# A two-layer trunk on one core: every large tile moved to a 512-byte place in SBUF

## The chip, the core and the metric

The kernel runs on one core of a Trainium2 chip. The core has a matrix engine (TensorE; PE in the profile, PEld for its loads of weights), a vector engine (DVE), a scalar engine (ACT), GpSimd (POOL), the queue of SyncE (SP) that issues most transfers, and 16 DMA engines between DRAM and the on-chip memory SBUF. SBUF has 128 partitions; a tile has the same byte address in all of them. The metric is the device time of one execution in microseconds (us), the median of several.

## What is computed

A context of 256 tokens and 256 latent tokens, 1024 features each, pass two layers. Each layer is a half-step SwiGLU, a token mixer (layer 0: RG-LRU; layer 1: gated DeltaNet), and another half-step SwiGLU, each behind an RMSNorm with shift and scale:

```python
def swiglu(h, w_in, w_out):
    gu = h @ w_in
    return (jax.nn.silu(gu[..., :D_FF]) * gu[..., D_FF:]) @ w_out

for i in range(DEPTH):
    x = x + 0.5 * m[:, 0, 2] * swiglu(adaln(x, g_sub[i, 0], m[:, 0]), ffn_w_in[i, 0], ffn_w_out[i, 0])
    ...
    o = mixer(h, hc)                  # RG-LRU, or gated DeltaNet in column-major order
    x = x + m[:, 1, 2] * o
    x = x + 0.5 * m[:, 2, 2] * swiglu(adaln(x, g_sub[i, 2], m[:, 2]), ffn_w_in[i, 1], ffn_w_out[i, 1])
return rms_norm(x, g_final)
```

All is float32, D_FF is 2816, and the context takes the same steps except at the very end. Nearly all the arithmetic is products of a [128 features, tokens] tile with [128, 128] tiles of weights.

## The kernel before

**Products.** A float32 operand is kept as two float32r parts, high and low (class HL). A product of tiles is three matrix products in `mm3`, lines 293 to 295: high weights with high data, high weights with low data, low weights with high data. The weights are the stationary operand, 128 columns, loaded anew for each product (one PEld row for each PE row). The data is the moving operand: 512 columns (context and latents) in most of the kernel, 256 columns where only one of the two is worked on.

**Stages, in order of time.** The start (up to some 62 us) works out the first modulation vectors; then come the first SwiGLU (to some 400 us), the RG-LRU (to 620), two more SwiGLUs (to 1346), DeltaNet's projections, chunked recurrence and readout (to 1707), and the last SwiGLU over the latents alone (to 1906). In the profile's names the input products of a SwiGLU are `gu<-hh,wp` and `gu<-hl,wp`, its output products `fo` and `tl` (from `hidh`, `hidl`), DeltaNet's projections `f<-H,wp`, and the output projections of the mixers `op` and `tl` (from `grh`, `grl`, and from `y`).

**Weights.** A tile of weights is loaded by SP into a raw tile `wr` (line 218). ACT writes its high half-tile by a cast into `wp` (line 157, in `split`), and DVE writes the low one as the difference (line 158). Raw tiles and pairs come from two rings (class `Ring`): ring g lives for the whole kernel (3 raw tiles, 8 pairs), and ring l belongs to a stage (2 raw tiles, 6 pairs). There are two stages with a ring l: from the first SwiGLU to the one before DeltaNet, and the last SwiGLU. The strings given to `WS.cycle` say in which order the two rings are drawn from.

**Working tiles.** `slot` hands out [128, 512] tiles of a stage's pool (`hh`, `hl`, `hn`, `hidh`, `hidl`, `hf`, `sg`, `sq`, `uhh`, `grh` and so on). DeltaNet's normed stream `H` has a pool of its own; its readout keeps `S`, `y`, `kt`, and the small `so`, `ro`, `rq`, `jk`.

**Order.** The order on each engine is partly written out (`manual_schedule`) and partly the work of the layer that records the program; where that layer knows of fewer buffers it can choose another order. Where a tile lies in SBUF follows from the order in which the pools first hand out their tiles and from the tiles' sizes. No line of the kernel before asks for a particular place.

Of the kernel before, what the change touches and what calls it, by code (L numbers as in the profile page):

```python
# [25 lines left out]
# how far the parts of the work that share the engines run apart  # L26
PACE = {
    # RG-LRU: the order of the tiles, u and y of the input projection, g the gates
    "lru": "u0 u1 u2 u3 u4 u5 g0 u6 u7 g1 y0 y1 y2 g2 y3 y4 y5 g3 y6 y7",
    # DeltaNet: the order of the projections after the keys  # L30
    "seq": "qqqqqqqqvvvvzzvzzvvzzvzz",
    # the projections at which the decays begin and have to be done, and the keys' blocks begin
    "decay_from": 6, "decay_to": 8, "keys_from": 9,
    # steps per tick of the work behind the projections, and pauses in it
    "steps": 4, "decay_steps": 1, "key_every": 4, "key_steps": 3, "solve": 4, "q_lag": 2, "v_lag": 6, "k_lag": 4,
    # parts of the diagonal, and of the other blocks that the vector engine lays out; GpSimd has the rest
    "block_split": 1, "mo": 2,
    # the last heads of the groups that the readout's norms go in, and heads read out ahead of the projection
    "readout": "1 3 5 7", "heads": 4,
    # tiles of weights ready ahead of the projections  # L40
    "ahead": 1,
    # tiles of DeltaNet's weights that are kept in two parts: all projections from one on, so many of the output's;
    # and the places of FFNs (which, part, turns) in which that is done
# [3 lines left out]
# columns of the array of small constants  # L47
# [9 lines left out]
# columns of the array of masks (they depend on shapes alone)  # L57
# [12 lines left out]
class HL:  # L70
    """A float32 operand as two float32r parts whose sum is exact."""
# [11 lines left out]
class Parts:  # L83
    """two tiles [128, 256], indexed by the columns of either like one [128, 512]"""
# [10 lines left out]
def trunk(ctx, tc, io):  # L95
# [16 lines left out]
    @contextmanager  # L112
    def phase(ns, nraw=0, nw=0):
        """room for ns working tiles, and for more weights: nraw as loaded, nw halves of each part"""
        with tc.tile_pool(name=nm("ph"), bufs=1, reuse_waits="tile") as p:
            old = dict(scope)
            scope.update(s=p, ns=ns)
            if nw:
                ring_l = Ring(p, "l", nraw, nw)
                WS.cycle("glglglglglglgg", "gggl" if nraw == 1 else "gglgl", ring_l)  # L120
            else:
                WS.cycle("g", "g", None)
            yield
            scope.clear()
            scope.update(old)
# [20 lines left out]
    # ---------------------------------------------------------------- constants  # L146
# [8 lines left out]
    # ---------------------------------------------------------------- helpers  # L155
# [4 lines left out]
    class Ring:  # L160
        """room for weights: nraw as loaded, nw halves of each part"""
# [11 lines left out]
    class Weights:  # L173
        """the weights in the order of their use: first some tiles on their way, then in two parts"""

        def __init__(self):
            self.plan, self.raw, self.ready, self.todo = deque(), deque(), deque(), deque()
            self.rings = {"g": Ring(sb, "g", 3, 8)}
            # tiles that are brought into two parts where the engines have room for it, and kept in DRAM till their use
# [44 lines left out]
        def want(self, n, deep=True):  # L224
            """n tiles are to be ready; first halves first"""
# [20 lines left out]
        def step(self, n=1):  # L246
            """the next n halves"""
            self.put()
            while n and self.todo:
                raw, a, b, ring, r, parts = self.todo.popleft()  # L250
                w = self.rings[r[0] if r else next(self.next_pair)].pair()
                if b - a == 256:  # the decays' and betas' weights, 32 columns of both parts side by side
                    v = w.hi[:, :512].rearrange("p (k u x) -> p u k x", u=2, x=32)
                    split(HL(v[:, 0], v[:, 1]), raw[:, a:b].rearrange("p (k x) -> p k x", x=32))
                else:
                    split(w[:, :b - a], raw[:, a:b])
# [21 lines left out]
        def pop(self):  # L278
            """f(column) -> [128, 128] of the parts of the next tile"""
# [17 lines left out]
    def rsqrt_steps(y, v, n, short=False):  # L297
        """y = 1/sqrt(v) for small tiles [128, n]; short: fewer steps, with the scalar engine's help"""
# [20 lines left out]
    def run(it, n=None):  # L319
        """n steps of a generator, or all"""  # L320
# [9 lines left out]
    # ---------------------------------------------------------------- stream  # L330
    V2 = (0, 1)                       # 0: context, 1: latent
# [10 lines left out]
    # ---------------------------------------------------------------- adaLN vectors  # L342
    M = {}

    def finish_m(l, q, m, vs=V2, ts=slice(0, 8)):
        """m [128, 8, 2] holds silu(c) @ w of vector q; add the bias, and bring it to the form it is used in"""
# [17 lines left out]
    cs2 = cs.rearrange("p (k v) -> p k v", v=2)  # L364
    adap = tc.alloc_tile_pool(name="adap", bufs=1)
# [12 lines left out]
    def ada_tile(q, t, m, raw):  # L378
        """tile t of vector q of layer 0 on the tensor engine, from the rows of w; a generator of two steps"""
# [5 lines left out]
        x = small("adx", 128, 4)  # L385
# [7 lines left out]
    def ada_dot(t, m, raw, vs=V2):  # L393
        """tile t of a layer's vectors, from the columns of w"""
# [5 lines left out]
    class Ada:  # L400
        """the vectors that are not needed at the very start, tile by tile behind the SwiGLUs"""
# [11 lines left out]
        def step(self, n):  # L413
            """n more tiles; what is left of a fraction is kept"""
# [18 lines left out]
    # ---------------------------------------------------------------- norm + modulation  # L433
    class Norm:
        """RMSNorm of the stream with its modulation, piece by piece"""

        def __init__(self, l, s, perm=False, short=False):
            """short: nothing else to do while the norms are worked out"""
# [7 lines left out]
        def add(self, d, v):  # L446
            """d, v of the stream is final"""
# [11 lines left out]
        def ss(self, v):  # L459
            """1 / rms of each token; a generator of single steps"""  # L460
# [12 lines left out]
        def rr(self, v):  # L473
            """the same on all partitions"""
# [5 lines left out]
        def h(self, k, v):  # L480
            """tile k of the result; a generator of its two steps"""
# [16 lines left out]
    def first(norm, W, P, vs=V2):  # L498
        """the first matrix products of a phase, behind the norm: the context, then the latents"""
# [41 lines left out]
    def first_whole(norm, W, P, vs):  # L541
        """the same for context and latents together, with what the norm itself asks for"""
# [11 lines left out]
    def tail(ds, take, l, q, norm, vs, between=lambda more: None, split_=2, ahead=4, res=residual):  # L554
        """the last products of a phase, take() -> f(bank, columns, n of parts, part): the context is done first"""
# [60 lines left out]
    # ---------------------------------------------------------------- SwiGLU  # L616
# [85 lines left out]
    # ---------------------------------------------------------------- small helpers  # L702
    def log1p_steps(out, e, n):
        """log(1 + e) for 0 <= e <= 1, by 2 atanh(e / (2 + e))"""
# [28 lines left out]
    def out_proj(x, l, q, cols, norm, perm=False, ahead=4, before=lambda k: None):  # L733
        """stream += gate * (x @ w) over all output tiles"""
# [33 lines left out]
    def pause(n):  # L768
        """room for the engines' own queues between a result and what another engine does with it"""
# [3 lines left out]
    def conv(u, p, cw, vs=V2, bias=0.0):  # L773
        """u = 4-tap convolution over the tokens of each part; p: PSUM bank; a generator of two steps, and pauses"""
# [11 lines left out]
    # ---------------------------------------------------------------- RG-LRU  # L786
    class Pipe:
        """work on earlier tiles, in small steps behind the matrix products"""
# [17 lines left out]
    def project(w, x, dst, cols, tick=lambda: None, every=2):  # L806
        """dst[cols] of a bank = one tile of output features"""
# [5 lines left out]
    class Lru:  # L813
# [10 lines left out]
        def prepare(self):  # L824
# [4 lines left out]
            # log a = -4 sp (1 + th), th the tanh of half the gate's argument  # L829
# [106 lines left out]
    # ---------------------------------------------------------------- gated DeltaNet  # L936
    # Tokens are cut into chunks of 64; chunk i lies on the half i % 2 of the partitions, in slot
    # (i // 2) ^ (i % 2), so that step s of both directions works on the two halves of one slot.
# [809 lines left out]
```

## Time and profile before

| | |
|---|---|
| runs | 1915.66, 1916.98, 1919.57 us; median 1916.98 us |
| profiled execution | span 1917.1 us (no separate time is listed for it) |
| PE busy | 1855.7 us, 97% |
| PEld busy | 1583.3 us |
| DVE busy | 1319.2 us |
| ACT busy | 803.6 us |
| POOL busy | 89.3 us |
| HBM traffic over the span | 156 GB/s |

The span is the time from the first to the last instruction of one execution. Matrix products overlap: a product's own time in the profile (0.28 us for 256 columns at full clock, 0.39 us for 512) is longer than the step from its start to the next one's start, and the ends are modelled. The text therefore reads steps between starts: the time between two starts divided by the number of products that begin in between. One column in each cycle of the 2.4 GHz clock would be a step of 106.7 ns for 256 columns and of 213.3 ns for 512. The column PEclk is the granted clock, 1.00 for 2.4 GHz; during a stretch of half clock the products follow each other at 1.2 GHz.

### The profile page before, as it was taken

How to read it: one execution, taken by the hardware profiler on the slowest of the kernel's cores; microseconds unless marked ns; L12 is line 12 of the kernel's file. 1: busy time of each engine (PE TensorE's matmuls, PEld its weight loads, DVE VectorE, ACT ScalarE, POOL GpSimd, SP SyncE). 2: the span in 40 equal slices, each digit the busy share in tenths (PEclk: the TensorE clock that was granted, in tenths of full speed). 3: DMA queues.
4: the chain of work that ended last, by engine and by line, in shares of the span. 5: the costliest groups of instructions: out<-in, count | busy, mean ns of one | idle time of the engine just before them, and what ended most of it. 6: DMA issues, size and time to landing. Idle time of an engine off the chain costs nothing.

```text
span 1917.1 us, 29208 instructions
## 1 busy us (share of the span) xinstructions
PE 1855.7 (97%) x11078; PEld 1583.3 (83%) x11078; DVE 1319.2 (69%) x2772; ACT 803.6 (42%) x1651; POOL 89.3 (5%) x130
## 2 busy tenths in 40 slices
PE   5999999999999999999999999999999989989998
PEld 3788888898779888888898888888988987789997
DVE  7867766787888768766466555546765976975555
ACT  5522133257874432233333323323554332854444
POOL 3100000000000000000000000000012330100000
PEclk9999999999999999999999999999987979989999
DMA  9344644442323766566326665644223550035553
GB/s 334 132 159 158 214 169 161 156 170 78 99 76 134 233 230 218 187 217 220 126 86 214 225 207 210 208 144 139 83 78 101 169 173 1 1 101 184 189 179 108
DMA packets 98061, 300.54 MB, mean 157 GB/s; under 512 B 10880, under 2 KB 20352, under 8 KB 97792
## 3 DMA queue, kind: packets, MB, share of 16 engines
q1 hardware_dynamic: 92160, 277.69, 42.7%
q0 software_dynamic: 5760, 20.97, 3.5%
q8 instruction: 87, 1.43, 0.3%
q14 instruction: 54, 0.44, 0.1%
HBM read 276.61 MB, written 22.02 MB: 156 GB/s over the span
## 4 chain that ended last, share of the span: by engine, by line
PE 83%; DVE 9%; issue 3%; ACT 3%; DMA 1%; POOL 0%; SPq 0%; POOLq 0%; ACTq 0%; DVEq 0%
PE gu L294 14%; PE gu L293 14%; PE gu L295 14%; PE fo L294 4%; PE fo L293 4%; PE fo L295 4%; PE tl L294 4%; PE tl L293 4%; PE tl L295 3%; PE p L1408 1%; DVE u L781 1%; PE p L1397 1%; PE f L293 1%; PE gr L1069 1%; PE f L295 1%
## 5 line engine op out<-in xcount | busy, mean ns | idle before, releaser
L157 ACT CAST wp<-wr 128x512 fp32r<-128x512 f32 (+1 forms) x689 | 383.0, 607 | 308.8 <-DMA wr<-in_ffn_out_dram 59.8
L158 DVE TENSOR_TENSOR wp<-wr,wp 128x512 fp32r<-128x512 f32 (+1 forms) x689 | 433.3, 674 | 104.5 <-ACT wp L157 100.8
L294 PE MATMUL gu<-hl,wp 128*128 128x512 f32 (+1 forms) x1312 | 488.3, 372 | 7.2 <-DVE hl L495 7.2
L293 PE MATMUL gu<-hh,wp 128*128 128x512 f32 (+1 forms) x1312 | 485.5, 370 | 0.0
L295 PE MATMUL gu<-hh,wp 128*128 128x512 f32 (+1 forms) x1312 | 481.1, 367 | 0.0
L294 PEld LDWEIGHTS gu<-hl,wp 128*128 128x128 f32 x1312 | 248.7, 190 | 52.4 <-DVE hl L495 9.5
L293 PEld LDWEIGHTS gu<-hh,wp 128*128 128x128 f32 x1312 | 248.6, 189 | 49.1 <-ACT m L390 0.8
L397 DVE SCALAR_TENSOR_TENSOR junk<-ar,cb 128x1024 bf16<-128x1024 f32 x224 | 273.8, 1222 | 21.6 <-DMA ar<-in_w_adaT_dram 17.7
L295 PEld LDWEIGHTS gu<-hh,wp 128*128 128x128 f32 x1312 | 249.3, 190 | 45.2
L647 ACT ACTIVATE sg<-gu 128x512 f32<-128x512 f32 (+1 forms) x88 | 47.9, 545 | 385.9 <-PE gu L295 376.0
L649 DVE TENSOR_TENSOR hf<-sg,gu 128x512 f32<-128x512 f32 (+1 forms) x88 | 54.6, 620 | 198.7 <-PE gu L295 149.3
L293 PE MATMUL tl<-hidh,wp 128*128 128x256 f32 (+1 forms) x418 | 140.5, 336 | 0.0
L294 PE MATMUL tl<-hidl,wp 128*128 128x256 f32 (+1 forms) x418 | 140.5, 336 | 0.0
L295 PE MATMUL tl<-hidh,wp 128*128 128x256 f32 (+1 forms) x418 | 139.5, 334 | 0.0
L294 PE MATMUL fo<-hidl,wp 128*128 128x512 f32 (+1 forms) x352 | 129.4, 368 | 0.0
L293 PE MATMUL fo<-hidh,wp 128*128 128x512 f32 (+1 forms) x352 | 128.6, 365 | 0.0
L295 PE MATMUL fo<-hidh,wp 128*128 128x512 f32 (+1 forms) x352 | 128.1, 364 | 0.0
L293 PE MATMUL f<-H,wp 128*128 128x256 f32 x320 | 96.5, 301 | 1.4 <-ACT sq L1040 1.2
L295 PE MATMUL f<-H,wp 128*128 128x256 f32 x320 | 95.1, 297 | 0.0
L294 PE MATMUL f<-H,wp 128*128 128x256 f32 x320 | 94.9, 296 | 0.0
L293 PEld LDWEIGHTS tl<-hidh,wp 128*128 128x128 f32 x418 | 79.1, 189 | 9.3
L294 PEld LDWEIGHTS tl<-hidl,wp 128*128 128x128 f32 x418 | 79.2, 190 | 8.4
(327 smaller groups left out, 2904.9 us busy)
## 6 DMA issues: line engine op xcount, KB each, us to landing
wr<-in_ffn_in_dram SPq DMA_DIRECT2D x172, 512.0 KB, 4.6
ar<-in_w_adaT_dram SPq DMA_DIRECT2D x128, 512.0 KB, 3.7
wr<-in_ffn_out_dram SPq DMA_DIRECT2D x64, 512.0 KB, 4.9
kp<-wp SPq DMA_DIRECT2D x80, 256.0 KB, 7.2
wp<-kp POOLq DMA_DIRECT2D x40, 512.0 KB, 4.9
wr<-in_dn_in_dram SPq DMA_DIRECT2D x32, 512.0 KB, 3.9
wr<-in_ffn_out_dram SPq DMA_DIRECT2D x64, 192.0 KB, 3.5
wr<-in_lru_in_dram SPq DMA_DIRECT2D x16, 512.0 KB, 3.8
```

The costliest lines, as they stand in the source:

```text
L157: ACT.copy(dst.hi, src)
L158: DVE.tensor_tensor(dst.lo, src, dst.hi.bitcast(F32), OP.subtract)
L293: PE.matmul(out, w.hi, x.hi, start=start, stop=False)
L294: PE.matmul(out, w.hi, x.lo, start=False, stop=False)
L295: PE.matmul(out, w.lo, x.hi, start=False, stop=stop)
L397: DVE.scalar_tensor_tensor(junk, raw, 1.0, cb[:, v], OP.mult, OP.mult, accum_out=m[:, t % 8, v:v + 1])
L647: ACT.activation(sg[:, cols], P[0][:, cols], AF.Silu)
L649: DVE.tensor_tensor(hf[:, cols], sg[:, cols], P[1][:, cols], OP.mult)
L781: DVE.scalar_tensor_tensor(uv[:, :, a:b], pv[:, :, a + sh:b + sh], cw(j), uv[:, :, a:b], OP.mult, OP.add)
L1069: PE.matmul(gr[HI, o], gc[HI, c:c + 1].to_broadcast([64, 64]), ident[HI, HI], start=True, stop=True)
L1397: PE.matmul(p2[:, 0:128], Yp[a][:, j * 8 + hd, :], rr, start=True, stop=True)
L1408: PE.matmul(p3[dr][:, 0:128], KT[hd][r2[dr], j * 128:j * 128 + 128], vs[r2[dr]], start=True, stop=True)
```

## The change

Empty tiles (`pad`), a few changed sizes, and tiles handed out once and dropped (`slot("first")`, `ring_l.pair()`, `ring_l.raw()`) move the addresses at which the pools' tiles begin. The copies of ring l and the working tiles are now laid out in a fixed order at a stage's start: working tiles, pairs, raw tiles. Two sets of small buffers shrink: `adx` from 4 to 3, `jk` from 2 to 1. `ea` gets 16 columns instead of 64, of which it used 16. All comments are removed, which moves the line numbers (line 293 becomes 297). What is computed, and by which instructions, is the same.

```diff
     def phase(ns, nraw=0, nw=0):
...
             scope.update(s=p, ns=ns)
             if nw:
+                slot("first")
+            if nw:
                 ring_l = Ring(p, "l", nraw, nw)
+                ring_l.pair()
+                ring_l.raw()
                 WS.cycle("glglglglglglgg", "gggl" if nraw == 1 else "gglgl", ring_l)
...
     cs2 = cs.rearrange("p (k v) -> p k v", v=2)
+    new_m()
+    sb.tile([128, 112], F32, name="pad")
     adap = tc.alloc_tile_pool(name="adap", bufs=1)
...
-        x = small("adx", 128, 4)
+        x = small("adx", 128, 3)
...
-        y, sg, g, ea = (one(n, [128, 64], hp) for n in ("y", "sg", "g", "ea"))
+        y, sg, g = (one(n, [128, 64], hp) for n in ("y", "sg", "g"))
+        ea = one("ea", [128, 16], hp)
...
         KQ, QK, VN, Z, KT = ({} for _ in range(5))
+        one("pad", [128, 16])
...
         so, ro, rq = (rg.tile([128, 8, 2], F32, name=n) for n in ("so", "ro", "rq"))
+        rg.tile([128, 72], F32, name="pad")
...
-                jk = small("jk", 128)
+                jk = small("jk", 128, 1)
```

The places, as bytes past a multiple of 512, follow from the addresses in the two built programs:

| tile | before | after |
|---|---|---|
| pairs of weights, ring g (`wp`) | 64 | 0 |
| pairs of weights, ring l, first stage with one | 416 | 0 |
| pairs of weights, ring l, last SwiGLU | 64 | 0 |
| raw weights (`wr`), ring g and ring l of the last SwiGLU | 64 | 0 |
| raw weights, ring l of the first stage | 160 | 0 |
| working tiles (`hh`, `hl`, `hidh`, `hidl`, `grh` ...), first stage | 160 | 0 |
| working tiles, last SwiGLU | 64 | 0 |
| DeltaNet's normed stream (`H`) | 0 | 0 |
| readout's `y` and `kt`; `S` | 288 | 0 |
| DeltaNet's other large tiles (`kq`, `qk`, `u`, `vn`) | 384 | 384 |

The slices of weights that a product loads are 512 bytes wide and begin at multiples of 512 bytes within their tile, so a product's weights lie at the place of their ring.

On PE the order of the products is the same except in DeltaNet's readout, where the first output products (`op`) run between transposes of the last heads' results (`yt`). Before, transposes of two heads came after the first four products:

```order
L293 MATMUL op_15794<-y_15764,wp_13850 128x256
L293 MATMUL op_15795<-y_15764,wp_13925 128x256
L293 MATMUL op_15796<-y_15764,wp_13970 128x256
L293 MATMUL op_15797<-y_15764,wp_15115 128x256
L1456 MATMUL yt_15776<-ident,vn_13376 128x128 x2
L1456 MATMUL yt_15785<-ident,vn_13468 128x128 x2
L294 MATMUL op_15794<-y_15764,wp_13850 128x256
L295 MATMUL op_15794<-y_15764,wp_13850 128x256
```

Now they come twelve and thirteen products later:

```order
L298 MATMUL op_15804<-y_15771,wp_15122 128x256
L299 MATMUL op_15804<-y_15771,wp_15122 128x256
L297 MATMUL op_15801<-y_15780,wp_13856 128x256
L298 MATMUL op_15801<-y_15780,wp_13856 128x256
L299 MATMUL op_15801<-y_15780,wp_13856 128x256
L297 MATMUL op_15802<-y_15780,wp_13931 128x256
L1465 MATMUL yt_15783<-ident,vn_13382 128x128 x2
L298 MATMUL op_15802<-y_15780,wp_13931 128x256
L1465 MATMUL yt_15792<-ident,vn_13474 128x128 x2
```

The transposes moved; the number of products and transposes is the same.

On ACT, just ahead of that, the squares of the readout's norms (`jk`, two for each head) stood as pairs between the recurrence's own instructions (`vn`, `oq`):

```order
L1403 ACTIVATE vn_15546<-p_15544,btc 128x128
L1390 ACTIVATE oq_15540<-p_15534,egf 64x128 x2
L1437 ACTIVATE jk_15551,so<-vn_13266 128x128
L1437 ACTIVATE jk_15553,so<-vn_13266 128x128
L1390 ACTIVATE oq_15561<-p_15555,egf 64x128 x2
L1403 ACTIVATE vn_15567<-p_15565,btc 128x128
L1437 ACTIVATE jk_15572,so<-vn_13316 128x128
L1437 ACTIVATE jk_15574,so<-vn_13316 128x128
```

With one buffer for `jk` the second square of a head comes an instruction or more after the first:

```order
L1411 ACTIVATE vn_15553<-p_15551,btc 128x128
L1398 ACTIVATE oq_15547<-p_15541,egf 64x128 x2
L1446 ACTIVATE jk_15558,so<-vn_13272 128x128
L1411 ACTIVATE vn_15574<-p_15572,btc 128x128
L1446 ACTIVATE jk_15560,so<-vn_13272 128x128
L1398 ACTIVATE oq_15568<-p_15562,egf 64x128 x2
L1446 ACTIVATE jk_15579,so<-vn_13322 128x128
L1398 ACTIVATE oq_15609<-p_15603,egf 64x128
```

The recurrence's `vn` of a step moved ahead of the second square. DVE's small instructions of the same norms moved by a few places in the same way, and GpSimd and SP have the same order as before.

## Rows read from the trace of the kernel before

**Rows 1.** The page: span, busy time by engine, the chain by engine.
```profile
span 1917.1 us, 29208 instructions
PE 1855.7 (97%) x11078; PEld 1583.3 (83%) x11078; DVE 1319.2 (69%) x2772; ACT 803.6 (42%) x1651; POOL 89.3 (5%) x130
...
PE 83%; DVE 9%; issue 3%; ACT 3%; DMA 1%; POOL 0%; SPq 0%; POOLq 0%; ACTq 0%; DVEq 0%
```

**Rows 2.** Busy time by window: stretch, length, engines, PEclk, DMA share, GB/s.
```profile
62.00:240.00 178.00, 178.00 (x767) 143.51 (x766) 133.01 (x245) 53.10 (x97) 0.00 (x0) 1.00 0.52 176
...
400.00:620.00 220.00, 213.79 (x1203) 183.72 (x1203) 178.28 (x359) 149.34 (x255) 0.00 (x0) 1.00 0.32 106
620.00:970.00 350.00, 350.00 (x1586) 286.09 (x1585) 229.89 (x399) 117.91 (x212) 0.00 (x0) 1.00 0.60 205
...
1719.00:1906.00 187.00, 187.00 (x1560) 187.00 (x1560) 106.12 (x194) 87.77 (x180) 0.00 (x0) 1.00 0.49 164
```

**Rows 3.** PE's products by line and shape: count, busy us, mean ns.
```profile
L294 PE MATMUL gu<-hl,wp 128*128 128x512 f32 x992 | 397.7, 401 | 7.2 <-DVE hl L495 7.2
...
L294 PE MATMUL fo<-hidl,wp 128*128 128x512 f32 x264 | 104.5, 396 | 0.0
...
L294 PE MATMUL f<-H,wp 128*128 128x256 f32 x320 | 94.9, 296 | 0.0
...
L294 PE MATMUL gu<-hl,wp 128*128 128x256 f32 x320 | 90.6, 283 | 0.0
...
L294 PE MATMUL tl<-hidl,wp 128*128 128x512 f32 x198 | 78.4, 396 | 0.0
...
L294 PE MATMUL tl<-hidl,wp 128*128 128x256 f32 x220 | 62.1, 282 | 0.0
...
L536 PE MATMUL gu<-hl,wp 128*128 128x256 f32 x160 | 26.5, 289 | 0.4 <-DVE hl L495 0.4
...
L294 PE MATMUL fo<-hidl,wp 128*128 128x256 f32 x88 | 24.9, 283 | 0.0
```

**Rows 4.** PE's timeline, 512 columns, data at 160, weights at 416 (ring l).
```profile
175.56 0.39 PE L295 MATMUL fo<-hidh,wp 128*128 128x512 f32 x1
...
181.00 0.40 PE L295 MATMUL fo<-hidh,wp 128*128 128x512 f32 x1
```

**Rows 5.** PE's timeline, 512 columns, data at 160, weights at 64 (ring g).
```profile
193.74 0.39 PE L293 MATMUL fo<-hidh,wp 128*128 128x512 f32 x1
...
204.24 0.40 PE L293 MATMUL fo<-hidh,wp 128*128 128x512 f32 x1
```

**Rows 6.** PE's timeline, 512 columns, data at 160, both rings in turn.
```profile
250.09 0.39 PE L293 MATMUL gu<-hh,wp 128*128 128x512 f32 x1
...
268.30 0.39 PE L293 MATMUL gu<-hh,wp 128*128 128x512 f32 x1
```

**Rows 7.** PE's timeline, 256 columns, data at 0 (H), weights at 64.
```profile
1387.49 0.28 PE L295 MATMUL f<-H,wp 128*128 128x256 f32 x1
...
1403.59 0.28 PE L293 MATMUL f<-H,wp 128*128 128x256 f32 x1
```

**Rows 8.** The same shape and places, a little earlier.
```profile
1356.65 0.28 PE L533 MATMUL f<-H,wp 128*128 128x256 f32 x1
...
1370.66 0.28 PE L988 MATMUL ab<-H,wp 128*64 128x256 f32 x1
```

**Rows 9.** PE's timeline of the last SwiGLU, 256 columns, data and weights at 64.
```profile
1719.10 0.28 PE L532 MATMUL gu<-hh,wp 128*128 128x256 f32 x1
...
1906.04 0.28 PE L464 MATMUL ss<-ones,acc 128*128 128x1 f32 x2
```

**Rows 10.** PE's timeline, 256 columns, data at 160, weights at 416.
```profile
1330.11 0.28 PE L294 MATMUL tl<-hidl,wp 128*128 128x256 f32 x1
...
1341.74 0.28 PE L295 MATMUL tl<-hidh,wp 128*128 128x256 f32 x1
```

**Rows 11.** PE's timeline at half clock, 256 columns, data and weights at 64.
```profile
1716.19 0.41 PE L532 MATMUL gu<-hh,wp 128*128 128x256 f32 x1
...
1717.90 1.05 PE L536 MATMUL gu<-hl,wp 128*128 128x256 f32 x4
```

**Rows 12.** One tile's instructions (duration ns min/median/max): low weights, squares.
```profile
L158 DVE TENSOR_TENSOR wp<-wr,wp x689: 426/685/1643, 18.4 to 1900.9; 128x512 fp32r<-128x512 f32 x157, 128x384 fp32r<-128x384 f32 x15, 128x256 fp32r<-128x256 f32 x1
...
L1437 ACT ACTIVATION_READ_ACCUMULATOR jk<-vn x16: 186/190/193, 1668.5 to 1680.2; 128x1 f32 x16
```

## The prediction

> **What bounds the kernel now.** I read the page's busy times first: PE is busy for 1855.7 of 1917.1 us, and the chain that ends last runs 83% over PE [rows 1]. The windows then show where this is plain: in the first SwiGLU (62 to 240 us), in the second layer-0 SwiGLU and what follows (620 to 970 us) and in the last SwiGLU (1719 to 1906 us) PE is busy for the whole of the window, at full clock, while DVE is busy for 133 of 178, 230 of 350 and 106 of 187 us and the DMA engines for 0.49 to 0.60 of the time [rows 2]. In such a stretch a product that follows the one before it sooner shortens the end by as much, as long as the weights keep up. In the RG-LRU (400 to 620 us) PE has idle time and DVE is busy for 178 of 220 us; there I count no gain.
>
> So the question is the step from one product to the next. Four stretches without a pause, all at full clock, show that it isn't one number for one shape:
> - 512 columns, data at 160, weights at 416: 24 products from 175.56 to 181.00 us, a step of 226.7 ns [rows 4].
> - 512 columns, data at 160, weights at 64: 45 products from 193.74 to 204.24, 233.3 ns [rows 5]; with the rings in turn 78 from 250.09 to 268.30, 233.5 ns [rows 6].
> - 256 columns, data at 0, weights at 64: 142 products from 1387.49 to 1403.59, 113.4 ns [rows 7], but 119 from 1356.65 to 1370.66, 117.7 ns [rows 8].
> - 256 columns, data and weights both at 64: 1558 products from 1719.10 to 1906.04, 120.0 ns [rows 9]; data at 160 and weights at 416: 97 from 1330.11 to 1341.74, 119.9 ns [rows 10].
>
> One column a cycle would be 213.3 and 106.7 ns. The lowest steps of both shapes stand to these as 17 to 16 (226.7 and 113.3 ns), the others as 17.5 or 18 to 16. At half clock the excess is gone: 8 products from 1716.19 to 1717.90 take 213.8 ns each, where one column a cycle is 213.3 [rows 11]. So what costs is the supply of operands, not the array, and it depends on where data and weights lie to each other or to a boundary. This is what the change moves.
>
> **Beside a page.** The row says that the same shape at the same clock takes 113.4 or 120.0 ns by place. The Trainium skill (SBUF — State Buffer, Who interferes with whom) says that PE never waits on anyone and that its two read ports are independent; by it the places of data and weights would change nothing, and the sum below would be zero. The trace disagrees with it by those 6.6 ns, so the zero gets a small chance of its own.
>
> **The change part by part.** All products keep their number; only places, and a few instructions of the readout, move.
>
> 512 columns. The large groups are 992 x 3 input products and (264 + 198) x 3 output products, 2976 and 1386 [rows 3]. The input products draw on both rings in turn, at 233.5 ns; half of the output products are at 233.3, half at 226.7 after a few slower ones when the ring changes. No row has data and weights at 0. The nearest is rows 4: there data and weights are a multiple of 256 apart, as they are at 0 and 0, and the step is 226.7. With that: 2976 x 6.8 ns = 20.2 us, and 693 x 6.6 ns = 4.6 us, plus about 1 us for the slower ones at ring changes: 25.8 us less. From both sides: 240.0 ns would be 18 to 16, as the 256-column rows with equal places have it; 220.0 ns would be the least if the excess of rows 7 (6.7 ns) is one for each product and not for each column.
>
> 256 columns. The last SwiGLU has 1558 at 120.0 [rows 9]. The others of `gu`, `tl` and `fo` are (320 + 160) x 3 + 220 x 3 + 88 x 3 = 2364 in all, less these: 806, at about 118 to 120 [rows 3, 10]. If they come to 113.3: 1558 x 6.7 = 10.4 us, 806 x 5.5 = 4.4 us. DeltaNet's projections (320 x 3) keep data at 0; their mean own time of 296 ns against 283 for products at a step of 120 holds stalls and the half-clock stretches, so I read them by rows 7 and 8: a quarter at 117.7 that come to 113.3, 240 x 4.4 = 1.1 us. Together 15.9 us. Here the bounds are far apart: the two rows with equal places (9 and 10) both stand at 120, the one with data at 0 at 113.4. I take 113.3, because data at 0 is the only row in which the products reach it, and in rows 9 and 10 the data begins off a 512-byte boundary; the other reading is the first rival.
>
> Vector and scalar engines. The low halves of weights take 685 ns in the median whichever ring they are of [rows 12], so I put DVE and ACT at no change. They run beside PE: in the first SwiGLU DVE has 45 us in 178 to spare [rows 2], and a PE that is 3% faster uses 6 of them. If that cover were gone, the gain would stop at DVE's 133 us for this window, which is far off.
>
> Loads. The order on SP is as before, and with it what is queued behind each load. In the last SwiGLU ring l's raw tiles now lie where DeltaNet's Yp and the readout's first `y` were, so the second of them waits for the last product that reads that `y`, which is done before the last SwiGLU's first product. The order of DMAs behind it on SP waits too. I take 0.5 us, with 0 and 3 us as bounds.
>
> Readout. With one buffer for `jk`, ACT's second square of a head waits for the first to be read out: 16 x 190 ns [rows 12] is 3.0 us at the most, on an engine that the recurrence's last steps wait for. Against it stands that the recurrence's own `vn` now goes ahead of the second square, which can give up to 8 x 190 ns = 1.5 us back. I take 0.5 us more, bounds -1.5 and 3. The transposes that move by twelve products cost nothing: their number is the same, and the heads that they serve come later in the row of products. `adx` with three buffers, `ea` with 16 columns and the pads issue nothing more.
>
> The sum: -25.8 - 15.9 + 0.5 + 0.5 = -40.7 us against the execution's 1917.1, which lies 0.1 us from the median. I round to 42 us less for the smaller groups of products that I left out, and predict 1875.
>
> **The rivals.**
> - *Equal places are the slow case for 256 columns.* Rows 9 and 10 have nothing in common but that data and weights are a multiple of 128 bytes apart, and both take 120; rows 7 have them 64 off. Then 512 columns go to 226.7 (rows 4 are such a case) and all 256-column products to 120, DeltaNet's too: 960 of these lose about 6 ns, 5.8 us, and the others about 1 us. -25.8 + 6.8 + 1 is -18, 1899 us. For it: it explains all rows but 8. Against: why 512 columns of the same places escape it.
> - *The excess is one for each product.* With data at 0 it is 6.7 ns in rows 7, with data off the boundary 13.3 in rows 4, 9 and 10, whatever the columns. Then 512 columns come to 220.0, another 4362 x 6.7 = 29 us: 1846, and 1838 with the smaller groups. For it: 13.3 in three rows of two shapes. Against: rows 5.
> - *The places don't matter to PE, or trade evenly:* 1917. For it: rows 7 and 8 differ at the same places, so history plays a part. Against: 1558 products at exactly 120.
> - *Slower:* equal places make both streams ask for the same part of SBUF in step, and what rows 9 show for 256 columns holds for 512 as well: 18 to 16, 240.0 ns. 2976 x 6.5 + 693 x 6.7 + 693 x 13.3 = 33 us, and 6 us for DeltaNet's projections: 1956. It decides as soon as the 512-column step is above some 232.4 ns, the present mean. Against it: rows 4.
> - *Lower than any row.* If supply stops being a limit, steps come near 213.3 and 106.7. No row is below 226.7 and 113.3 at full clock, but none has weights at 0; 4362 x 10 ns and 3324 x 4 ns more would make 1818. The Trainium skill (TensorE: Matmul & The Clock Gate, Back-to-back issue gap) gives N/2.4 + 2.5 ns, 215.8 and 109.2, for back-to-back products; the trace has none so short.
>
> **How the numbers follow.** Forecast 0.33, equal places slow 0.20, one excess a product 0.22, lower than any row 0.05: faster in all four, 0.80. No matter 0.08. Slower 0.12. A measurement can tell about 0.2% (4 us) from no change; each case lies on one side of that. The range reaches from below the second rival to no change, 1830 to 1917, which leaves out the lowest case, the slower one and part of no matter, some 0.2.
>
> **What would show it.** In the profile after: the first SwiGLU's output products at one step for both rings, near 226.7 (forecast, first rival), 220 (second), 240 (slower); the last SwiGLU at 113.3 over its whole length, 176.5 us instead of 186.9, or at 120 still; DeltaNet's projections at 113.4 throughout, or at 120. DVE's and ACT's durations should be as before, and PE's idle time in the readout within 2 us. The prediction is wrong if the step depends on something that no place sets, such as the phase after a stall, or if PE's gain comes back as waits for weights.

## The result, and the profile after

The changed kernel takes 1894.78 us in the median (1890.98 to 1897.33) beside 1917.01 us for the kernel before on the same chip, a ratio of 0.9876 [0.9862, 0.9890]. The profiled execution spans 1892.8 us, 24.3 less than in [rows 1]. So it is faster, by a little more than half of the forecast 42 us, and inside the range.

The page after: span, busy time by engine, the chain by engine.
```profile
span 1892.8 us, 29201 instructions
PE 1827.7 (97%) x11078; PEld 1585.6 (84%) x11078; DVE 1316.6 (70%) x2772; ACT 803.3 (42%) x1651; POOL 89.5 (5%) x130
...
PE 86%; DVE 6%; issue 4%; ACT 3%; DMA 1%; POOL 0%; SPq 0%; POOLq 0%; DVEq 0%; ACTq 0%
```
PE lost 28.0 us of busy time, DVE and ACT 2.6 and 0.3. PE still bounds the kernel, and a little more so than in [rows 1].

PE's timeline of after (start, duration, what; lines 297 to 299 are 293 to 295 of before): the first and the last product of unbroken stretches, first two of 512 columns, then DeltaNet's projections, then the last SwiGLU.
```profile
62.72 0.39 PE L299 MATMUL gu<-hh,wp 128*128 128x512 f32 x1
...
390.06 0.28 PE L297 MATMUL tl<-hidh,wp 128*128 128x256 f32 x1
...
619.20 0.40 PE L297 MATMUL gu<-hh,wp 128*128 128x512 f32 x1
...
941.54 0.28 PE L297 MATMUL tl<-hidh,wp 128*128 128x256 f32 x1
...
1362.89 0.28 PE L298 MATMUL f<-H,wp 128*128 128x256 f32 x1
...
1380.17 0.28 PE L298 MATMUL f<-H,wp 128*128 128x256 f32 x1
...
1693.60 0.28 PE L538 MATMUL gu<-hh,wp 128*128 128x256 f32 x1
...
1881.51 0.17 PE L470 MATMUL ss<-ones,acc 128*128 128x1 f32 x1
```
The steps, worked out as ahead of the prediction: 1444 products from 62.72 to 390.06 are 226.7 ns each, 1422 from 619.20 to 941.54 are 226.7. `gu`, `fo` and `tl` with weights of both rings lie in these stretches, so the 233.3 and 233.5 of [rows 5, 6] are gone. The projections' 144 from 1362.89 take 120.0 ns where [rows 7] had 113.4. The last SwiGLU's 1566 from 1693.60 take 120.0, exactly as in [rows 9].

The same by line and shape (count, busy us, mean ns of a product's own time), against [rows 3]: the 512-column products (`fo`) are shorter, `f` is longer, the last SwiGLU's form (`gu` of 256 columns) is the same.
```profile
L298 PE MATMUL fo<-hidl,wp 128*128 128x512 f32 x264 | 102.7, 389 | 0.0
...
L298 PE MATMUL f<-H,wp 128*128 128x256 f32 x320 | 96.2, 301 | 0.0
...
L298 PE MATMUL gu<-hl,wp 128*128 128x256 f32 x320 | 90.6, 283 | 0.0
```

Where the time went, by three marks of PE's timelines (the projections' first product, their last, the last SwiGLU's first) and the end of the span; a second profile of each kernel beside the first:

| stretch, us | before | before, 2nd | after | after, 2nd |
|---|---|---|---|---|
| start to the projections' first product | 1347.4 | 1349.1 | 1321.9 | 1321.5 |
| projections, first to last product | 211.9 | 209.5 | 216.0 | 215.8 |
| recurrence and readout, to the last SwiGLU's first product | 154.2 | 153.4 | 151.7 | 151.8 |
| last SwiGLU to the end | 203.6 | 203.5 | 203.2 | 203.8 |

Of the 24.3 us, 25.5 come before the projections, where the 512-column products are. The projections give back 4.1, the last SwiGLU, where 10.4 were forecast, gives 0.4, and 2.5 come from the recurrence and readout. The second pair of profiles gives 27.6, loses 6.3 and 0.3, and gives 1.6, so each of these is good to some 2 us. Over the projections the granted clock was 0.90 or 0.91 in all four, so what they lost is not a lower clock. Of the 25.5, 1.0 came in the RG-LRU, which the first `u` and the next SwiGLU's first product bound (415.41 to 602.62 us before, 407.59 to 593.82 after).

### The profile page after: what moved, and what is told of

Read it like the earlier page. It is cut to its first block, busy times and chain, and to the rows that moved or that the text cites. A ratio compares the mean times of both kernels' runs of the same rounds, so it can differ in the third digit from the quotient of the medians.

```text
span 1892.8 us, 29201 instructions
## 1 busy us (share of the span) xinstructions
PE 1827.7 (97%) x11078; PEld 1585.6 (84%) x11078; DVE 1316.6 (70%) x2772; ACT 803.3 (42%) x1651; POOL 89.5 (5%) x130
## 4 chain that ended last, share of the span: by engine, by line
PE 86%; DVE 6%; issue 4%; ACT 3%; DMA 1%; POOL 0%; SPq 0%; POOLq 0%; DVEq 0%; ACTq 0%
PE gu L298 14%; PE gu L299 14%; PE gu L297 14%; PE fo L297 4%; PE fo L299 4%; PE fo L298 4%; PE tl L297 4%; PE tl L298 4%; PE tl L299 4%; PE f L297 2%; PE f L298 2%; PE f L299 2%; PE p L1416 1%; PE p L1405 1%; DVE hl L501 1%
## 5 line engine op out<-in xcount | busy, mean ns | idle before, releaser
L298 PE MATMUL gu<-hl,wp 128*128 128x512 f32 (+1 forms) x1312 | 479.7, 366 | 9.2 <-DVE hl L501 9.2
L297 PE MATMUL f<-H,wp 128*128 128x256 f32 x320 | 98.0, 306 | 1.4 <-ACT sq L1048 1.1
L299 PE MATMUL f<-H,wp 128*128 128x256 f32 x320 | 96.3, 301 | 0.0
L298 PE MATMUL f<-H,wp 128*128 128x256 f32 x320 | 96.2, 301 | 0.0
```

What stands on the lines that cost most here:

```text
L297: PE.matmul(out, w.hi, x.hi, start=start, stop=False)
L298: PE.matmul(out, w.hi, x.lo, start=False, stop=False)
L299: PE.matmul(out, w.lo, x.hi, start=False, stop=stop)
```

## The experiments

The first profile after says that the first rival's steps came true, but not why. Places are written here as (data, weights), in bytes past a multiple of 512; "difference" is data minus weights. Two theories stood at the start. **Difference**: the step follows from where data and weights lie to each other. **Boundary**: each operand wants its own 512-byte place, whatever the other does.

**Weights alone off the boundary.** Data stay at 0, both rings' pairs go to 64. (`pre` and `mid` are empty tiles of so many bytes, ahead of a stage's working tiles and ahead of its ring l.)
```diff
-    sb.tile([128, 112], F32, name="pad")
...
+    adap.tile([128, 112], F32, name="pada")
...
+        dns.tile([128, 112], F32, name="padd")
...
+    with eng("PS"), phase(44, 2, 6, mid=64):
+    with eng("PADGS"), phase(44, 2, 6, pre=448, mid=64):
```


> The changed kernel, but both rings of weights, raw tiles and pairs, lie at 64 bytes past a multiple of 512 in every stage; data stay at 0. Theory D (the difference between the place of the data and that of the weights, modulo 128 bytes, sets the step): all 256-column products leave 120 ns for 113.3 to 117.7 ns, the last SwiGLU loses 10 us, DeltaNet's projections 3 to 6 us, the other 256-column products about 4 us. For 512 columns no run so far has a difference of 64; if it is as good as 0 they stay at 226.7 ns and the whole comes to about 1875 us, if it is as bad as 32 or 96 they go to 233.3 ns and the whole to about 1903 us. Theory B (each operand wants its own 512-byte boundary, and what is off it costs): 512 columns go back to 231 to 233 ns, 256 columns stay at 120 or more, the whole is 1915 us or more.

Measured: 1909.02 us, ratio 0.9949 [0.9933, 0.9965]. PE's timeline, one 512-column stretch and the last SwiGLU:
```profile
628.93 0.40 PE L301 MATMUL gu<-hh,wp 128*128 128x512 f32 x1
...
960.74 0.28 PE L301 MATMUL tl<-hidh,wp 128*128 128x256 f32 x1
...
1713.75 0.28 PE L543 MATMUL gu<-hh,wp 128*128 128x256 f32 x1
...
1891.81 0.16 PE L474 MATMUL ss<-ones,acc 128*128 128x1 f32 x1
```
1422 products at 233.3 ns, and 1571 of the last SwiGLU at 113.3: the two shapes go opposite ways. 512 columns lose what the change gave them, and 256 columns reach the step that the prediction had hoped for at equal places.

**Everything off the boundary together.** One pad less moves weights and all working tiles to 64 (only the readout's `y` stays at 0).
```diff
-    sb.tile([128, 112], F32, name="pad")
```


> The changed kernel with everything, data and weights alike, moved to 64 bytes past a multiple of 512 (only the readout's y stays at 0). Theory D: nothing changes, 512 columns at 226.7 ns, 256 columns at 120.0, 1895 us within 3 us. Theory B: every product has both operands off the boundary, 512 columns go to 231 to 240 ns and the whole back to 1915 us or above.

Measured: 1897.78 us, ratio 0.9892 [0.9871, 0.9913]. PE's timeline, 512 columns and projections:
```profile
619.05 0.40 PE L297 MATMUL gu<-hh,wp 128*128 128x512 f32 x1
...
941.43 0.28 PE L297 MATMUL tl<-hidh,wp 128*128 128x256 f32 x1
...
1362.76 0.28 PE L298 MATMUL f<-H,wp 128*128 128x256 f32 x1
...
1380.04 0.28 PE L298 MATMUL f<-H,wp 128*128 128x256 f32 x1
```
226.7 and 120.0 ns, the steps of the changed kernel, with nothing on a 512-byte place. The boundary theory falls; equal places are what the change gives.

**Weights at 96** (as the first, with pads for 96; one run).


> The changed kernel, but both rings of weights at 96 bytes past a multiple of 512; data at 0. Theory D: the difference is 96, as in the kernel before where data were at 160 and weights at 64 (-96): 512 columns at 233.3 ns, 256 columns at a mix of 116 to 125 ns, the whole near 1920 us. Theory B: 512 columns off 226.7 too, with data on the boundary as in the first run of this set, so both runs with moved weights give the same 512-column step.

Measured: 1919.79 us.
```profile
631.47 0.39 PE L301 MATMUL gu<-hh,wp 128*128 128x512 f32 x1
...
964.62 0.28 PE L301 MATMUL tl<-hidh,wp 128*128 128x256 f32 x1
```
1422 products at 234.3 ns; 256 columns between 117.3 and 118.7 by stretch. 512 columns are slower than at 64, and no 256-column stretch comes near 113.3.

**Weights at 128** (pads for 128; one run). The kernel before had steps of 226.7 and 120 at a difference of 256 too [rows 4, 10], so I held that 128 might count as equal.


> As the changed kernel, but with both rings' pairs of weights at 128 instead of 0 (data at 0). Difference of the places modulo 128: as the changed kernel, 512 columns at 226.7, 256 at 120.0, about 1895. Modulo 256 or 512: 512 columns slower than 226.7 (233.3 as with 64 and 96), 256 below 120: 1905 to 1920.

Measured: 1919.34 us, beside 1921.37 for the kernel before. PE's timeline, 512 columns and the last SwiGLU:
```profile
629.78 0.39 PE L301 MATMUL gu<-hh,wp 128*128 128x512 f32 x1
...
961.58 0.28 PE L301 MATMUL tl<-hidh,wp 128*128 128x256 f32 x1
...
1720.67 0.28 PE L547 MATMUL gu<-hl,wp 128*128 128x256 f32 x1
...
1906.26 0.17 PE L475 MATMUL ss<-ones,acc 128*128 128x1 f32 x1
```
233.3 and 118.7 ns (a later 512-column stretch, 1422 products from 1002.14 to 1332.58, has 232.4). So 128 isn't equal; 0 and 256 are. "A multiple of 128 apart" in the first rival's wording was wrong, though it changed nothing there.

**256-column groups 64 apart, 512-column groups equal.** From the changed kernel: `H` goes to 448 and the last SwiGLU's working tiles to 64, weights stay at 0.
```diff
-        one("pad", [128, 16])
...
-    with eng("PADGS"), phase(44, 2, 6):
+    with eng("PADGS"), phase(44, 2, 6, pre=64, mid=448):
```


> The changed kernel with weights at 0, and the data alone moved in two stages: DeltaNet's normed stream to 448 and the last SwiGLU's working tiles to 64, so that data and weights are 64 bytes apart modulo 128 there. All else as changed. Theory D: the last SwiGLU goes from 120.0 to 113.3 ns a product, 10.4 us less, or to 117.7 and 3.6 us less; DeltaNet's projections lose 2 to 6 us; the whole 1879 to 1889 us. Theory B: data off the boundary gain nothing, both stages at 120 or above, 1895 us or more.

Measured: 1891.13 us, ratio 0.9859 [0.9833, 0.9885], short of what was expected. PE's timeline of the last SwiGLU:
```profile
1695.71 0.28 PE L543 MATMUL gu<-hh,wp 128*128 128x256 f32 x1
...
1880.03 0.28 PE L474 MATMUL ss<-ones,acc 128*128 128x1 f32 x2
```
1565 products at 117.8 ns without a break, neither 120.0 nor 113.3; the projections, at 448, stood at 113.4 in most of their stretches. Their whole stage still took 216.0 us, as in the changed kernel: its granted clock was 0.87 here and 0.91 there, so this stage's length does not show the shorter step. [rows 7, 8] had shown both 113.4 and 117.7 at one pair of places. So a difference of 64 has two steps, and a stream keeps the one that it is in. What chooses?

**One narrow product, then ten of several shapes.** In [rows 8] the projections change from 117.7 to 113.4 behind products with 64 columns of weights (`ab`). So I put one such product into the last SwiGLU, and in a further kernel ten, one at every second hidden tile; the next product overwrites their results.
```diff
+                    if vs != V2 and j == 2:
+                        PE.matmul(P[0][:64, cols], W[0](0).hi[:, :64], h[0][:, cols].hi, start=True, stop=True)
```


> As e4_h (weights at 0, DeltaNet's stream at 448, the last SwiGLU's working tiles at 64), with one product put in: before the first product of the third hidden tile in the last SwiGLU, one with 64 columns of weights and 256 of data, whose result the next product overwrites. History theory (at a difference of 64 bytes a 256-column stream has two states, 113.3 and 117.7 ns, and keeps the one that it falls into until it is disturbed; in DeltaNet's projections it fell into 113.3 right behind such narrow products): the 1417 or so products behind the new one go from 117.7 to 113.3, 6.2 us less than e4_h: about 1885, the new product itself costs 0.1. Rival, place alone (117.7 belongs to data at 64 with weights at 0, 113.3 to data at 448 with weights at 0): still 117.7 to the end, 1891.

> As e4_h, with ten such products in the last SwiGLU, one ahead of every second hidden tile, of several shapes (64 or 32 columns of weights; 64, 128 or 192 columns of data with all of the weights). History theory: the step changes between 113.3 and 117.7 at some of these places and nowhere else, so that the last SwiGLU is a chain of stretches at either; a time between 1885 and 1892. Place alone: 117.7 in all stretches, some 1892.

Measured: 1889.27 us, ratio 0.9845 [0.9821, 0.9869], and 1887.11 in the one run with ten. PE's timelines, the whole last SwiGLU of the first, and of the second a part from one inserted product to a later one:
```profile
1688.68 0.28 PE L543 MATMUL gu<-hh,wp 128*128 128x256 f32 x1
...
1873.59 0.28 PE L474 MATMUL ss<-ones,acc 128*128 128x1 f32 x2
```
```profile
1743.59 0.25 PE L677 MATMUL gu<-hh,wp 128*128 128x192 f32 x1
1743.68 0.30 PE L301 MATMUL gu<-hh,wp 128*128 128x256 f32 x1
1743.82 0.28 PE L302 MATMUL gu<-hl,wp 128*128 128x256 f32 x1
...
1797.52 0.22 PE L677 MATMUL gu<-hh,wp 128*64 128x128 f32 x1
```
1570 products at 117.8 with one inserted; 456 at 117.8 from 1743.82 to 1797.52, with a third inserted product among them (at 1786.10), and 117.8 in each of the other stretches. The disturbance breaks the rhythm for a product or two and the stream falls back to where it was. History, in this form, is refuted.

The start still matters. In the kernel with one inserted product the projections have the places and the order of the kernel without it, and yet the stretch that ends at the first `ab` has another step. Without, then with (one profile of each):
```profile
1331.53 0.28 PE L543 MATMUL f<-H,wp 128*128 128x256 f32 x1
...
1345.55 0.28 PE L999 MATMUL ab<-H,wp 128*64 128x256 f32 x1
```
```profile
1333.12 0.28 PE L543 MATMUL f<-H,wp 128*128 128x256 f32 x1
...
1346.61 0.28 PE L1001 MATMUL ab<-H,wp 128*64 128x256 f32 x1
```
119 products each, at 117.8 ns and at 113.4. So at a difference of 64 neither the places nor the program's order fix the step; what does is not shown.

**The sign.** What was left: the projections at 113.4 have their data 64 *below* the weights' place, the last SwiGLU at 117.8 has it 64 *above*. Two kernels as mirror images: projections, readout's output products and last SwiGLU with data at 448, or at 64, weights at 0, 512-column groups equal; and the changed kernel again beside them.
```diff
-        one("pad", [128, 16])
...
-        rg.tile([128, 72], F32, name="pad")
+        rg.tile([128, 88], F32, name="pad")
...
-    with eng("PADGS"), phase(44, 2, 6):
+    with eng("PADGS"), phase(44, 2, 6, pre=448, mid=64):
```


> Weights at 0, and all data that is only worked on with 256 columns from the projections on (DeltaNet's stream, the readout's output products, the last SwiGLU) at 448, that is 64 bytes below the weights' place; the 512-column tiles stay at 0 as in the changed kernel. Sign theory (data 64 bytes below the weights' place: mostly 113.3 ns; 64 above: 117.7): the last SwiGLU's 1566 products at 113.3 over most of its length, 6 to 7 us less than e4_h and e5_one (1889 to 1891): 1882 to 1885, the readout's 360 products 2 us less still at best. Rival (the state at a difference of 64 either way is chance at the stretch's start, and the last SwiGLU's start falls into 117.7): 117.7 to the end again, 1888 to 1891.

> The mirror image of e8_minus: the same groups of data at 64, that is 64 bytes above the weights' place. Sign theory: DeltaNet's projections, which took 113.3 for the greater part at 448, take 117.7 throughout (960 products, up to 4 us more than e4_h), the last SwiGLU 117.7: 1893 to 1895. Rival (chance): projections mostly at 113.3 as in e4_h, 1889 to 1891.

> The changed kernel once more, beside the two others on the same chip: 1895 within 3, ratio 0.988. No theory differs on it; it is the mark for the other two.

Measured: 1881.04 us with data below, ratio 0.9812 [0.9787, 0.9837]; 1886.74 above, 0.9825 [0.9798, 0.9851]; the changed kernel 1894.12, 0.9873 [0.9849, 0.9897]. PE's timeline of the last SwiGLU with data below:
```profile
1697.23 0.28 PE L543 MATMUL gu<-hh,wp 128*128 128x256 f32 x1
...
1874.84 0.28 PE L474 MATMUL ss<-ones,acc 128*128 128x1 f32 x2
```
And with data above, two stretches of the projections and the last SwiGLU:
```profile
1332.26 0.28 PE L543 MATMUL f<-H,wp 128*128 128x256 f32 x1
...
1360.82 0.28 PE L303 MATMUL f<-H,wp 128*128 128x256 f32 x1
...
1506.15 0.28 PE L302 MATMUL f<-H,wp 128*128 128x256 f32 x1
...
1517.34 0.27 PE L1186 MATMUL tv<-ident,vs 128*128 128x128 f32 x1
...
1691.09 0.28 PE L546 MATMUL gu<-hl,wp 128*128 128x256 f32 x1
...
1875.29 0.28 PE L474 MATMUL ss<-ones,acc 128*128 128x1 f32 x2
```
Below: 1567 products at 113.3 ns. Above: 1564 at 117.8, and the projections' later stretches at 117.8 (95 from 1506.15). From its first product to the end the last SwiGLU takes 192.7 us below and 199.9 above. The sign goes with the step of the last SwiGLU in all six kernels: 113.3 in the two with data 64 below (here and in the first experiment), 117.8 in the four above. It isn't a law: above, 252 products of the projections from 1332.26 (32 of them `ab`) stand at 113.3; below, some stretches of the projections stay at 117.7 [rows 8], and so did the readout's output products of the first experiment. What fixes these exceptions stays open. The kernel with data at 448 beats the kernel before and the changed one, this by 13.1 us. Its lead over the mirror image is not shown by the times, since the two intervals overlap; the profiles show it in the last SwiGLU alone. The profile with data below is of the slowest of five executions (1887.90 us, the fastest 1878.72) and holds a pause in the second SwiGLU, where no place differs from the changed kernel's (the bracket is PE's idle time and what ended it):
```profile
726.30 0.50 PE L301 MATMUL fo<-hidh,wp 128*128 128x512 f32 x1 [1.48 <-ACT hidh L165]
```
From 726 to 731 us the granted clock was 0.68, and the projections begin at 1326.8 us instead of 1321.9. The mirror image was forecast at 1893 to 1895 by the sign and came out at 1886.7: I had added 4 us for the projections, but their stretch took 211.5 us, no longer than the 212.9 with data below, since 4 ns on some 600 products are 2.4 us, and two kernels with `H` at 448 and the same order took 216.0 and 209.8 us for that stretch.

**The order of the readout alone.** One edit in the kernel before gives the changed kernel's order on every engine, with all large tiles at the places of before; and the kernel before once more.
```diff
-                jk = small("jk", 128)
+                jk = small("jk", 128, 1)
```


> The kernel before with one edit: one buffer for jk instead of two. All places of the tiles that products read are as before, and the order on every engine is that of the changed kernel. Prediction's term: +0.5 us (bounds -1.5 and 3), a ratio of 1.0003. Rival, read from the two profiles (from the last projection product to the last SwiGLU's first product 154.2 us before, 151.7 after): the new order is worth 2.5 us less, ratio 0.9987, with that stretch at 151.5 to 152.5. If the places alone make the gain, the whole change's ratio of 0.988 has no part here.

> The kernel before, unchanged, for a second profile of it: how far the stretch from the last projection product to the last SwiGLU's first product (154.2 us in the first profile) and the projections (211.9) move from one execution to another. Prediction's term: 154 within 0.5. Rival (this stretch spreads by itself): off by 1 us or more.

Measured: 1918.96 us beside 1920.14, ratio 0.9994 [0.9981, 1.0007]; the kernel before 1917.25 in its one run. PE's timelines, the last projection product and the last SwiGLU's first: kernel before; its second profile; the edit; the changed kernel (the bracket is PE's idle time and what ended it).
```profile
1559.29 0.28 PE L295 MATMUL f<-H,wp 128*128 128x256 f32 x1
...
1713.46 0.58 PE L532 MATMUL gu<-hh,wp 128*128 128x256 f32 x1 [1.11 <-ACT hh L493]
```
```profile
1558.64 0.28 PE L295 MATMUL f<-H,wp 128*128 128x256 f32 x1
...
1712.03 0.58 PE L532 MATMUL gu<-hh,wp 128*128 128x256 f32 x1 [1.11 <-ACT hh L493]
```
```profile
1560.65 0.28 PE L295 MATMUL f<-H,wp 128*128 128x256 f32 x1
...
1714.40 0.58 PE L532 MATMUL gu<-hh,wp 128*128 128x256 f32 x1 [1.11 <-ACT hh L493]
```
```profile
1537.92 0.28 PE L299 MATMUL f<-H,wp 128*128 128x256 f32 x1
...
1689.60 0.58 PE L538 MATMUL gu<-hh,wp 128*128 128x256 f32 x1 [1.11 <-ACT hh L499]
```
154.2, 153.4, 153.7 and 151.7 us. The new order alone doesn't give the 2.5 us, and its ratio covers no change. In the kernels with the new order and moved tiles the stretch takes 151.4 to 153.7 us, so about 2 us is what it spreads by, and the 2.5 are not to be explained by the order. Whether the places give a part of them stays open.

## Why the prediction was right, and where it was not

- **512 columns, -25.8 us: right.** The step went to 226.7 in every long stretch, and the marks give 25.5 us up to the projections, 24.5 without the RG-LRU, where the prediction counted no gain. The choice of [rows 4] as the nearest row was sound, and the second experiment says why: 256 apart, in stretches of one ring, and equal give one step.
- **256 columns, -15.9 us: wrong, and it is the step that failed.** It read the two 120.0 rows as "data off a boundary" and the 113.4 row as "data on it". The other reading, written down as the first rival, was the true one: equal places (or 256 apart) cost 120.0, and `H` at 0 was fast because its weights lay 64 further. The changed kernel made `H` equal too, so the projections went up from 113 or 118 ns to 120 and lost 4.1 us, and the last SwiGLU gained nothing. The rule used, that the only row to reach a value shows its condition, was weak: [rows 7] differed from [rows 9] in two things at once, the data's place and the difference, and the trace held no row that parted them. The first experiment did, in one kernel.
- **The first rival, 1899 us: right in the steps**, and 4 us off the median, since it charged the projections 5.8 where the marks show 4.1, and the recurrence and readout came out 2.5 shorter in this pair of profiles.
- **No change on DVE and ACT: right.** The low halves of weights, one tile's instructions (duration ns min/median/max), as [rows 12] had them with 685:
```profile
L162 DVE TENSOR_TENSOR wp<-wr,wp x689: 426/684/1750, 17.4 to 1876.3; 128x512 fp32r<-128x512 f32 x157, 128x384 fp32r<-128x384 f32 x15, 128x256 fp32r<-128x256 f32 x1
```
- **Cover by DVE, loads +0.5: the cover held, the loads cost nothing.** Windows of after (length, then PE, PEld, DVE, ACT, POOL busy, PEclk, DMA share, GB/s):
```profile
62.00:240.00 178.00, 178.00 (x787) 147.44 (x786) 134.71 (x248) 56.28 (x102) 0.00 (x0) 1.00 0.54 183
...
1695.00:1880.00 185.00, 185.00 (x1544) 185.00 (x1543) 106.23 (x194) 87.74 (x180) 0.00 (x0) 1.00 0.50 166
```
 In the first 178 us PE gets 787 products done where [rows 2] had 767, and DVE is busy for 1.7 us more. In the last SwiGLU PE is busy all the time, so no load is late.
- **Readout +0.5: no effect that can be told**, 0.9994 [0.9981, 1.0007] by the edit alone.
- **The other rivals** fell with one row each: no 512-column stretch at 220 or 240, none below 226.7, and places do matter.

The sum closes: 42 forecast less 24.3 seen is 17.7. 15.9 did not come at the 256-column products, 4.1 were lost in the projections, 1.3 was rounding for small groups that gained nothing, 0.3 came short up to the projections; against it stand the 1.0 charged for loads and readout that did not arise, 2.5 in the recurrence and readout, and 0.4 at the end. The terms are those of the first pair of profiles, and the second pair would shift some by 2 us.

That the time fell inside the range is in part luck. The range was laid wide, down to the second rival and up to no change, and it took in the first rival, which is what came; of the two parts of the forecast one came in full and the other not at all. The step from "the excess is gone at half clock" to "the supply of operands costs, not the array" was argued: the runs bear out that it is gone (last section), and show nothing of the supply itself. And the 117.7 of [rows 8] is 17.7 to 16, neither 17.5 nor 18, though no term used that.

**Beside a page.** The step of one shape at one clock went from 233.3 to 226.7 ns when nothing but the place of its operands was moved. The Trainium skill (SBUF — State Buffer, Who interferes with whom) has PE wait on no one and its two read ports independent. The runs disagree with the independence for float32r products, by 6.6 ns of 512 columns and 6.7 of 256: with data at 0, 256 columns take 120.0 ns beside weights at 0 and 113.3 beside weights at 64, with data at 64 they take 117.8 and 120.0, so neither operand's place sets the step by itself. Whether the ports are the cause no run shows.

## What to carry to other kernels

Where PE is busy without a pause, read the step between starts for each pair of places, and vary the place of one operand alone before choosing places for all: here one rule for all tiles gave some 23 us (ratio 0.9876), and a place by shape (512 columns equal, the 256 columns from the projections on with data 64 below the weights) some 36 (ratio 0.9812). When two rows of a trace differ in two things, the reading that needs fewer exceptions across all rows is worth a run before it is worth a forecast.

## What the runs showed of the hardware

For float32r products with 128 columns of weights at full clock, by difference of data and weights (bytes; ns per product):

| difference | 512 columns | 256 columns |
|---|---|---|
| 0 (both at 0, or both at 64) | 226.7 | 120.0 |
| 256 | 226.7 in stretches of one ring [rows 4], 233.7 where the rings take turns [rows 6] | 119.9 [rows 10] |
| -64 | 233.3 | 113.3, in some stretches 117.7 |
| +64 | not run | 117.8, one part of the projections at 113.3 |
| -96 | 234.3 | 117.3 to 118.7 |
| +96 | 233.3 [rows 5] | not read apart |
| 128 | 233.3, in some stretches 232.4 | 118.7 |

I had not expected that the two shapes want opposite places, nor that one pair of places has two steady steps which a stream keeps through more than 1500 products and finds again after a disturbance. No stretch of either shape at full clock went below 17/16 of the time of one column a cycle (226.7 and 113.3 ns).

At half clock these places make no difference. In unbroken stretches of DeltaNet's projections at a granted clock of 0.50 a 256-column product takes 213 to 214 ns, one column a cycle, at a difference of 0 (22 steps from 1398.55 to 1403.24 us of the changed kernel), of -64 (20 from 1397.66 to 1401.93 of the kernel with `H` at 448 and the last SwiGLU at 64) and of +64 (20 from 1396.54 to 1400.81 of the mirror image).

Why the shapes differ, and how sign and start choose between 113.3 and 117.8, the runs don't say.
